# Two transformer blocks on one core: block 2's products at 512 columns, full-row scores, one root at the entry, the selector's units last, and norm 2 in pairs

## The chip, the cores and the metric

The kernel runs on one core of one Trainium2 chip. The metric is device microseconds of one execution of the whole program. The kernel before took 2176.15, 2176.34 and 2179.45 us in three runs; the median is 2176.34 us.

## The reference

Everything is fp32; there are 256 tokens of width 2048. Block 1 is one layer: eight stick-breaking heads (sb), eight sparse heads (dsa) whose keys a small indexer selects, and a gated FFN with a causal convolution of width 3 and inner width 5504. Block 2 is two layers, each with three kinds of attention on one normalized input: six "fox" heads (a forget gate), six "mla" heads (low-rank, with a 64-wide rope part that all heads share) and four "diff" heads (two 64-wide maps each, subtracted); each output is gated, and one product leads back to width 2048. Cut to the lines that the change touches:

```python
h = rmsnorm(x, norm1_g[l]) * (1.0 + sc1) + sh1
rel = jax.nn.relu(jnp.einsum('bqhd,bkd->bqhk', q_idx[:, start:end], k_idx[:, :L]))   # 16 indexer heads of 64
_, sel = lax.top_k(score, topk)
x = x + g1 * (merged @ w_out[l])
h2 = rmsnorm(x, norm2_g[l]) * (1.0 + sc2) + sh2
x = x + g2 * conv_ffn(h2, w_up[l], conv_w[l], conv_b[l], w_down[l])
# block 2, mla: 128 + 64 rows per score
s = (jnp.einsum('bqhd,bkhd->bhqk', q_nope[:, q0:q1], k_nope[:, :q1])
     + jnp.einsum('bqhr,bkr->bhqk', q_rope[:, q0:q1], k_rope[:, :q1]))
# block 2, diff: two maps of 64 rows
s1 = jnp.einsum('bqhd,bkhd->bhqk', q1[:, q0:q1_], k1[:, :q1_]).astype(jnp.float32) * scale + bias
s2 = jnp.einsum('bqhd,bkhd->bhqk', q2[:, q0:q1_], k2[:, :q1_]).astype(jnp.float32) * scale + bias
```

## The kernel before

Weights come from HBM in steps of 512 KB (128 rows by 1024 columns). For accuracy each is split on the chip into a high and a low part: ACT copies the high part (`wh`, L1731), DVE subtracts for the low part (`wl`, L1740). Activations have such pairs too (`a0h`, `a0l` and so on). A product of a 128x128 weight block with 256 tokens is three matmuls of 256 columns: wh with the high part, wh with the low part, wl with the high part (`mm_feature`, L516; `mm_token`, L537, for values with tokens in the rows). I call these three, for one block of 128 rows (k) and one of 128 columns (m), a pair. In the FFN `mm_halves` makes a pair of one matmul of 512 columns (wh with high and low side by side, L527) and one of 256 (L528). A unit is 256 output columns with all 16 row blocks, so 32 pairs in four steps; it fills one of two PSUM banks named `mm`, which ACT or DVE empties one step later.

Stages by time in the profiled execution: input product of block 1 20 to 365 us, output product 368 to 479, norm 2 479 to 489, FFN 489 to 1219, block 2's layer 0 1219 to about 1690, layer 1 to 2158, and the final norm.

Attention is side work: generators on three lanes (PSUM tiles `l0a`, `l0b`, `l1a` ...), each of which issues one part of its work between two steps of the products. An engine runs its instructions in the order written, so a matmul of a side job that waits holds up the products behind it. `IN_PASSES` sets in which order the units of block 1's input product are finished: the indexer's (0 to 5), the dsa queries (5 to 10), the sb heads.

Places that the change touches: `scores` (L786) issues a head's score products, for 128 tokens against 128 keys and for 128 against 256; mla adds a second pair for the 64 rows of `krd` and `qr`. `indexer` L744 does 64-row products, two tiles side by side. `h2_tiles` (L1098 to L1100) makes the input of the FFN from `xa`, which ACT scales at L1076. `first_rs` runs at block 2's entry: two sums of squares (L606, L607) and two chained inverse roots, since block 1's final norm and block 2's first norm follow on each other. `fm_evac` (L1372, L1374) empties a unit's bank in one DVE operation of 512 columns.

## Time and profile before

| | |
|---|---|
| median of three runs | 2176.34 us |
| the profiled execution: time, span | 2171.6 us, 2169.8 us |
| TensorE (PE) busy | 2118.1 us (98%) |
| VectorE (DVE) busy | 1514.3 us (70%) |
| ScalarE (ACT) busy | 1138.9 us (52%) |
| GpSimd (POOL) busy | 91.0 us (4%) |
| HBM | 211 GB/s over the span |

Busy time of matmuls overlaps from one to the next, so the pace is read from the distance of two starts, not from the length of one. A row of the timeline gives start, length, engine, line, operation, tiles and shape; consecutive alike instructions share a row, and a bracket at its end tells how long the engine had been idle before it and on whose work it waited.

### The profile page before, as it was taken

The page shows a single profiled execution, that of the slowest core. Times are in us where ns is not written, and L with a number is a line of the kernel's source. Part 1 is how long each engine was busy: PE and PEld are TensorE (multiplying, and loading weights), DVE is VectorE, ACT ScalarE, POOL GpSimd, SP SyncE. Part 2 cuts the span into 40 slices and gives each one's busy share as a digit, 9 for nine tenths or more (in the row PEclk, how much of TensorE's full clock was granted, in tenths as well). Part 3 has the DMA queues.
Part 4 walks back from the last instruction along what each step waited for, and adds up shares of the span by engine and source line. Part 5 has one row for each costly group of instructions (what it writes and reads, how often), then busy time and mean ns, then how long its engine had stood idle before and what let it go on. Part 6 is the DMA issues. An engine that isn't in the chain of part 4 may idle for free.

```text
span 2169.8 us, 39066 instructions
## 1 busy us (share of the span) xinstructions
PE 2118.1 (98%) x15435; PEld 1958.2 (90%) x15435; DVE 1514.3 (70%) x2495; ACT 1138.9 (52%) x1810; POOL 91.0 (4%) x87
## 2 busy tenths in 40 slices
PE   8999899999999999999999999999999999999997
PEld 6898789988888888888888899998999999998997
DVE  8596858989988678877778855476555545675654
ACT  5876446444565455535555535464544444554543
POOL 0000000011200000000001200000001100000000
PEclk9999999999999999999999999999999999999999
DMA  9999687777855777776655555544455655544552
GB/s 344 357 358 359 222 305 255 249 260 282 273 193 185 227 225 234 231 244 224 199 175 184 166 186 169 174 135 152 147 179 157 200 184 159 161 131 146 178 182 98
DMA packets 131821, 460.48 MB, mean 212 GB/s; under 512 B 15655, under 2 KB 17591, under 8 KB 131637
## 3 DMA queue, kind: packets, MB, share of 16 engines
q1 hardware_dynamic: 128736, 453.27, 62.8%
q0 software_dynamic: 2176, 4.30, 0.8%
q8 instruction: 121, 1.98, 0.4%
q14 instruction: 64, 0.52, 0.1%
q10 hardware_dynamic: 724, 0.41, 0.1%
HBM read 455.80 MB, written 2.90 MB: 211 GB/s over the span
## 4 chain that ended last, share of the span: by engine, by line
PE 50%; DVE 2%; issue 1%; ACT 0%; DMA 0%; POOL 0%; DVEq 0%; ACTq 0%; POOLq 0%
PE mm L516 32%; PE mm L537 6%; PE mm L527 3%; PE l1b L527 2%; PE l1a L527 2%; PE mm L528 1%; PE l1a L528 1%; PE l1b L528 1%; DVE wl L1740 1%; PE l0a L786 1%; PE l2a L786 1%; PE l1a L786 1%; DMA t<-t5d 0%; DVE XT L1675 0%; ACT l_t L778 0%
## 5 line engine op out<-in xcount | busy, mean ns | idle before, releaser
L1740 DVE TENSOR_TENSOR wl<-raw,wh 128x1024 fp32r<-128x1024 f32 (+4 forms) x697 | 830.7, 1198 | 443.6 <-PE mm L516 216.3
L1731 ACT ACTIVATE wh<-raw 128x1024 fp32r<-128x1024 f32 (+4 forms) x697 | 705.3, 1017 | 624.9 <-PE mm L516 276.2
L456 DVE CUSTOM_DVE_ANT_0 ada<-ada,CROW 128x1024 f32<-128x1024 f32 x128 | 156.1, 1227 | 3.8 <-DMA ada<-in_weights_dram 3.6
L516 PE MATMUL mm<-mix,wh 128*128 128x256 f32 x512 | 93.6, 285 | 0.3 <-DVE wo L1063 0.3
L516 PEld LDWEIGHTS mm<-mix,wh 128*128 128x128 f32 x512 | 79.8, 192 | 0.5 <-issue 0.4
L516 PE MATMUL mm<-mix,wl 128*128 128x256 f32 x256 | 72.6, 284 | 1.2 <-DVE wl L1740 1.2
L778 ACT ACTIVATE l_t<-l_t,l_mx 128x128 f32<-128x128 f32 x96 | 43.0, 448 | 51.0 <-DVE l_mx L776 51.0
L516 PE MATMUL mm<-a6h,wh 128*128 128x256 f32 (+2 forms) x242 | 52.2, 297 | 0.0
L516 PE MATMUL mm<-a4h,wh 128*128 128x256 f32 (+2 forms) x242 | 50.4, 299 | 1.3 <-ACT mm L985 1.1
L1050 POOL COPY sqacc<-sq 128x512 f32<-128x512 f32 x4 | 4.0, 990 | 1111.1 <-ACT sq L1045 1111.1
L516 PEld LDWEIGHTS mm<-mix,wl 128*128 128x128 f32 x256 | 49.0, 192 | 1.6 <-DVE wl L1740 1.6
L1052 POOL TENSOR_TENSOR sqacc<-sqacc,sq 128x512 f32<-128x512 f32 x25 | 40.4, 1617 | 203.8 <-ACT sq L1045 203.8
L516 PE MATMUL mm<-a7l,wh 128*128 128x256 f32 (+2 forms) x242 | 48.7, 283 | 0.0
L516 PE MATMUL mm<-a7h,wh 128*128 128x256 f32 (+2 forms) x242 | 48.7, 283 | 0.0
L516 PE MATMUL mm<-a6l,wh 128*128 128x256 f32 (+2 forms) x242 | 48.7, 283 | 0.0
L516 PE MATMUL mm<-a5l,wh 128*128 128x256 f32 (+2 forms) x242 | 47.1, 284 | 0.5 <-ACT a5l L646 0.4
L516 PE MATMUL mm<-a5h,wh 128*128 128x256 f32 (+2 forms) x242 | 47.1, 285 | 0.0
L516 PE MATMUL mm<-a4l,wh 128*128 128x256 f32 (+2 forms) x242 | 47.0, 285 | 0.0
L516 PEld LDWEIGHTS mm<-a4h,wh 128*128 128x128 f32 (+2 forms) x242 | 37.9, 189 | 4.3 <-ACT mm L985 1.9
L1162 ACT ACTIVATE fy<-fu,PC 128x256 f32<-128x256 f32 x60 | 32.8, 594 | 15.1 <-DVE fu L1138 15.1
L516 PEld LDWEIGHTS mm<-a6h,wh 128*128 128x128 f32 (+2 forms) x242 | 37.7, 190 | 3.2 <-issue 1.6
L516 PEld LDWEIGHTS mm<-a5l,wh 128*128 128x128 f32 (+2 forms) x242 | 37.9, 192 | 1.0 <-ACT a5l L646 0.6
(1512 smaller groups left out, 6751.8 us busy)
## 6 DMA issues: line engine op xcount, KB each, us to landing
raw<-in_weights_dram SPq DMA_DIRECT2D x638, 512.0 KB, 4.0
ada<-in_weights_dram SPq DMA_DIRECT2D x192, 512.0 KB, 5.2
raw<-in_weights_dram SPq DMA_DIRECT2D x30, 256.0 KB, 2.6
raw<-in_weights_dram SPq DMA_DIRECT2D x8, 384.0 KB, 3.1
XT<-in_x_dram SPq DMA_DIRECT2D x4, 512.0 KB, 6.1
out_dram<-XT SPq DMA_DIRECT2D x8, 256.0 KB, 2.4
l_t<-nd POOLq DMA_DIRECT2D x12, 128.0 KB, 4.9
raw<-in_weights_dram SPq DMA_DIRECT2D x8, 140.0 KB, 2.1
```

The lines of the kernel that those rows point to most:

```text
L456: DVE.tensor_tensor_reduce(raw, raw, CROW[:, 1024 * g : 1024 * (g + 1)], 1.0, 0.0, ALU.mult, ALU.add, SUMS[:, h, j, g : g + 1])
L516: PE.matmul(o, a[:, j, wsl], b, start=first and j == 0 and m == 0 and x == 0, stop=last and j == len(ks) - 1 and x == 2, skip_group_check= ...
L527: PE.matmul(ps[0][m], wh[:, j, msl], act.both(ks[j]), start=first and j == 0, stop=False, skip_group_check=True)
L528: PE.matmul(ps[0][m][:, 1, :], wl[:, j, msl], act.H(ks[j]), start=False, stop=end, skip_group_check=True)
L537: PE.matmul(ps[0][:, tt, :n], a[:, tsl], b[:, j, :n], start=first and j == 0 and tt == 0 and x == 0, stop=last and j == len(ks) - 1 and x ...
L778: ACT.activation(Pt[:, a:b], Pt[:, a:b], AF.Exp, bias=mx[:, qt : qt + 1], scale=-1.0, accum_out=sm[:, qt : qt + 1])
L786: PE.matmul(z[:, a:b], q[:, qt * P : (qt + 1) * P], k[:, : b - a], start=x == 0, stop=x == len(pairs) - 1)
L1050: nc.gpsimd.tensor_copy(acc, sq)
L1052: nc.gpsimd.tensor_tensor(acc, acc, sq, ALU.add)
L1162: ACT.activation(y[:, m], ps[:, m, :], AF.Identity, bias=col("conv_b", c), scale=col("conv_w2", c))
L1731: ACT.activation(h, a, AF.Copy)
L1740: DVE.tensor_tensor(l, a, h.bitcast(F32), ALU.subtract)
```

## The change

- Block 2's products of the queries, keys, low-rank parts, gates and outputs (all units of feature form but the small one and `aq0`: 20 a layer, and 8 of `wo`) become `half_unit`: first all 16 row blocks of columns 0 to 127, then those of 128 to 255. Each pair is one matmul of 512 and one of 256 columns, and each half has a bank of its own, which `half_evac` empties in three operations of 256 columns.
- Scores in 128 rows: for mla and diff ACT copies the query with one half of its rows multiplied by zero, and the key stays whole; the indexer's key is stored twice with zeros in the other half. In block 1 the two products of value tile 0 become one.
- `first_rs` takes one root for the product of both norms, and spawns two steps later.
- The units of the selector are finished last in block 1's input product; the dsa heads wait for them.
- Norm 2: `xa` is scaled by POOL instead of ACT; `h2_tiles` goes by pairs, on DVE alone, in place.

```diff
--- before.py
+++ after.py
-             (0, 5, 8, 12, "put"), (17, 22, 4, 8, "put"), (5, 10, 8, 12, "put"), (0, 5, 12, 16, "put"), (5, 10, 12, 16, "put"), (10, 17, 8, 16, "put"), (17, 22, 8, 16, "put"))
+             (0, 5, 8, 12, "put"), (17, 22, 4, 8, "put"), (5, 10, 8, 12, "put"), (5, 10, 12, 16, "put"), (0, 5, 12, 16, "put"), (10, 17, 8, 16, "put"), (17, 22, 8, 16, "put"))
...
-H2_TILES = (0, 4, 5, 8)
+H2_TILES = (0, 4, 6, 8)
...
+    HALVES = [kcol[:, 4 + j : 5 + j] for j in range(2)]
...
+    def mm_half(ps, act, ks, first, last):
+        def go(wh, wl):
+            h, l = (w.rearrange("p k n -> p (k n)").rearrange("p (k n) -> p k n", n=P) for w in (wh, wl))
+            for j, k in enumerate(ks):
+                PE.matmul(ps[0], h[:, j, :], act.both(k), start=first and j == 0, stop=False, skip_group_check=True)
+                PE.matmul(ps[0][:, 1, :], l[:, j, :], act.H(k), start=False, stop=last and j == len(ks) - 1, skip_group_check=True)
+        return go
+    def half_unit(loads, ks, act, evac, pre=None):
+        for m in range(2):
+            ps = [None]
+            at = [(max(o, m * P), o, w, name, row, c) for o, w, name, row, c in loads if o < (m + 1) * P and o + w > m * P]
+            for i in range(0, len(ks), 8):
+                pk = ks[i : i + 8]
+                first, last = i == 0, i + 8 >= len(ks)
+                core = mm_half(ps, act, pk, first, last)
+                def mm(wh, wl, ps=ps, first=first, core=core):
+                    if first:
+                        ps[0] = pp.tile([P, 2, T], F32, tag="mm", bufs=2, name="mm")
+                    core(wh, wl)
+                parts = [(len(pk), P, [(a - m * P, min(o + w, (m + 1) * P) - a, name, row + pk[0] * P, c + a - o) for a, o, w, name, row, c in at])]
+                steps.append(Step(parts, mm, (lambda ps=ps, m=m: evac(ps[0], m)) if last else None, pre if m == 0 and i == 0 else None))
...
+        for j in range(2):
+            DVE.memset(kix[rows[1 - j], j, :], 0.0)
...
-                    po = 64 * j
-                    PE.matmul(ps[j][:, m, :n], S[f"qix{g}"][po : po + 64, m, tsl], kix[po : po + 64, :n], start=True, stop=True)
+                    PE.matmul(ps[j][:, m, :n], S[f"qix{g}"][:, m, tsl], kix[:, j, :n], start=True, stop=True)
...
-        PE.matmul(o[:, 0:P], v(0), PT[:, 0, :], start=True, stop=True)
-        PE.matmul(o[:, P:T], v(0), PT[:, 1, :], start=True, stop=False)
-        PE.matmul(o[:, P:T], v(1), PT[:, 2, :], start=False, stop=True)
+        PE.matmul(o, v(0), PT[:, 0:2, :].rearrange("p a b -> p (a b)"), start=True, stop=False, skip_group_check=True)
+        PE.matmul(o[:, P:T], v(1), PT[:, 2, :], start=False, stop=True, skip_group_check=True)
...
+            side.spawn("dsa", lambda L, h=h: dsa_head(L, h), after=("rds", "qix", "idx"))
...
-                        ACT.activation(G["xa"][k // 2][:, k % 2], XT[:, k, :], AF.Copy, scale=a2[:, k : k + 1])
+                        nc.gpsimd.tensor_scalar(G["xa"][k // 2][:, k % 2], XT[:, k, :], a2[:, k : k + 1], None, op0=ALU.mult)
...
-        for k in range(lo, hi):
-            t = ring("ht", (P, T))
-            (nc.gpsimd if k % 2 else DVE).tensor_tensor(t, G["xa"][k // 2][:, k % 2], G["RS2"], ALU.mult)
-            ACT.activation(H2.H(k), t, AF.Identity, bias=mod(3, k))
-            DVE.scalar_tensor_tensor(H2.L(k), t, mod(3, k), H2.H(k).bitcast(F32), op0=ALU.add, op1=ALU.subtract)
+        for k0 in range(lo, hi, 2):
+            xa, rs = G["xa"][k0 // 2], G["RS2"]
+            if k0 == 0:
+                for j in range(2):
+                    DVE.tensor_tensor(xa[:, j], xa[:, j], rs, ALU.mult)
+                    ACT.activation(H2.H(j), xa[:, j], AF.Identity, bias=mod(3, j))
+            else:
+                DVE.tensor_tensor(xa, xa, b2(rs), ALU.mult)
+                for j in range(2):
+                    ACT.activation(H2.H(k0 + j), xa[:, j], AF.Identity, bias=mod(3, k0 + j))
+            for j in range(2):
+                DVE.scalar_tensor_tensor(H2.L(k0 + j), xa[:, j], mod(3, k0 + j), H2.H(k0 + j).bitcast(F32), op0=ALU.add, op1=ALU.subtract)
...
+        RSX = G["rsx"] = cp.tile([P, T], F32, tag="RSa", name="RSX")
+        m1, m2 = L.sb("t2", [P, T]), L.sb("t3", [P, T])
+        ACT.copy(m1, ps)
+        DVE.scalar_tensor_tensor(m2, m1, EPS, ps2, op0=ALU.mult, op1=ALU.add)
+        rsqrt(L, RSX, m2, D, squared=True)
         r1 = cp.tile([P, T], F32, tag="RSb", name="r1")
-        rsqrt(L, r1, ps, D)
-        q = L.sb("t2", [P, T])
-        DVE.tensor_tensor(q, r1, r1, ALU.mult)
-        yield
-        r2 = cp.tile([P, T], F32, tag="RSc", name="r2")
-        RSX = G["rsx"] = cp.tile([P, T], F32, tag="RSa", name="RSX")
-        rsqrt(L, r2, ps2, D, pre=q)
-        DVE.tensor_tensor(RSX, r1, r2, ALU.mult)
         side.spawn("rsc", lambda L: rs_cols(L, RSX, rsx, 3), after=("rsx",))
-        side.spawn("x2", lambda L: second_x(L, r1))
+        side.spawn("x2", lambda L: second_x(L, r1), after=("rsx",))
+        yield
+        rsqrt(L, r1, m1, D)
...
+        def half_evac(name, i, RS, scale=None, then=None):
+            def ev(ps, m):
+                if m == 0:
+                    S2[name] = i() if callable(i) else slot(i, name)
+                s = S2[name]
+                t = ring("half", (P, T))
+                ACT.activation(t, ps[:, 0, :], AF.Copy, scale=1.0 if scale is None else scale)
+                if scale is None:
+                    DVE.tensor_tensor(t, ps[:, 1, :], t, ALU.add)
+                else:
+                    DVE.scalar_tensor_tensor(t, ps[:, 1, :], scale, t, op0=ALU.mult, op1=ALU.add)
+                DVE.tensor_tensor(s[:, m], t, RS(), ALU.mult)
+                if then and m == 1:
+                    then(s)
+            return ev
...
-            po = slice(64 * (h % 2), 64 * (h % 2) + 64)
-            qr = S2[f"qr{h // 4}"][po, (h // 2) % 2, :]
+            qr = L.sb("t1", [P, T])
+            ACT.activation(qr, S2[f"qr{h // 4}"][:, (h // 2) % 2, :], AF.Copy, scale=HALVES[h % 2])
+            yield
             z = L.ps("a", [P, 384])
-            scores(z, [(qn[:, h % 2, :], kn), (qr, S2["krd"][po])])
+            scores(z, [(qn[:, h % 2, :], kn), (qr, S2["krd"])])
...
+            qz = L.sb("t1", [P, 2, T])
+            for j in range(2):
+                ACT.activation(qz[:, j], q[:, h % 2, :], AF.Copy, scale=HALVES[j])
+            yield
             for j in range(2):
                 z = L.ps("ab"[j], [P, 384])
-                po = slice(64 * j, 64 * j + 64)
-                scores(z, [(q[po, h % 2, :], k[po, h % 2, :])])
+                scores(z, [(qz[:, j], k[:, h % 2, :])])
...
-             pre=lambda: (opened(), side.spawn("rsx", first_rs if l == 0 else layer_rs)), pre_at=3, delay=3)
+             pre=opened, pre_at=3, delay=3)
         for j in range(3):
-            unit(mat(W, O_AQ + 256 * j, 256), 256, kd, H, fm_evac(f"aq{j}", j, RSX, scale=P**-0.5))
+            if j == 0:
+                unit(mat(W, O_AQ, 256), 256, kd, H, fm_evac("aq0", 0, RSX, scale=P**-0.5),
+                     pre=lambda: side.spawn("rsx", first_rs if l == 0 else layer_rs), pre_at=1)
+                continue
+            half_unit(mat(W, O_AQ + 256 * j, 256), kd, H, half_evac(f"aq{j}", j, RSX, scale=P**-0.5))
...
-            unit(mat(W, off + 256 * j, 256), 256, kd, H, fm_evac(f"g{i}", WHERE[i], RSX, then=then), pre=pre)
+            half_unit(mat(W, off + 256 * j, 256), kd, H, half_evac(f"g{i}", WHERE[i], RSX, then=then), pre=pre)
...
+                def ev(ps, j):
+                    m = 2 * u + j
+                    for h in range(2):
+                        DVE.tensor_tensor(XT[:, m, :], XT[:, m, :], ps[:, h, :], ALU.add)
+                    split((XA[1].H(m), XA[1].L(m)), XT[:, m, :], scale=col("norm_g_2", 16 + m))
+                    if j:
+                        add_sq(sq1, XT[:, 2 * u : 2 * u + 2, :], u)
                 return ev
...
-                unit(mat(WO, 256 * u_, 256), 256, kd, M, wo_evac(u_), pre=wait_gates if u_ == 0 else None)
+                half_unit(mat(WO, 256 * u_, 256), kd, M, wo_evac(u_), pre=wait_gates if u_ == 0 else None)
```

On PE at block 2's entry, before: `sqacc`, `sq` are the sums of squares that POOL folds, `a0h` to `a7l` the input tiles, and the 70-column unit is the small one.

```order
L516 MATMUL mm<-a5h,wl 70x256
L516 MATMUL mm<-a5l,wh 70x256 x2
L516 MATMUL mm<-a5l,wl 70x256
L606 MATMUL l0b<-sqacc,ones 128x256
L607 MATMUL l0b<-sqacc,ones 128x256
L606 MATMUL l0a<-sq_122,ones 128x256
L607 MATMUL l0a<-sq_122,ones 128x256
L516 MATMUL mm<-a6h,wh 70x256 x2
L516 MATMUL mm<-a6h,wl 70x256
```

After, the small unit's end runs straight into `aq0`:

```order
L520 MATMUL mm<-a7h,wl 70x256
L520 MATMUL mm<-a7l,wh 70x256 x2
L520 MATMUL mm<-a7l,wl 70x256
L520 MATMUL mm<-a0h,wh 128x256 x2
L520 MATMUL mm<-a0h,wl 128x256
```

And, still after, the end of the first step of `aq0` with the products of `first_rs`:

```order
L520 MATMUL mm<-a1l,wh 128x256 x2
L520 MATMUL mm<-a1l,wl 128x256
L637 MATMUL l0b<-sqacc,ones 128x256
L638 MATMUL l0b<-sqacc,ones 128x256
L637 MATMUL l0a<-sq_127,ones 128x256
L638 MATMUL l0a<-sq_127,ones 128x256
L520 MATMUL mm<-a2h,wh 128x256 x2
L520 MATMUL mm<-a2h,wl 128x256
```

The four products with `ones` stood ahead of the last two of the small unit's eight pairs of tiles in its last step, and now stand behind the first step of `aq0`.

On PE around the first mla score of a layer, before (`kn`, `qn` are the key and query of 128 rows, `krd`, `qr` the rope parts in 64):

```order
L537 MATMUL mm<-wh,m5l 128x256 x2
L537 MATMUL mm<-wl,m5l 128x256
L786 MATMUL l1a<-kn_15972,qn_15822 128x128
L786 MATMUL l1a<-krd,qr_15921 128x128
L786 MATMUL l1a<-kn_15972,qn_15822 128x256
L786 MATMUL l1a<-krd,qr_15921 128x256
L516 MATMUL mm<-a0h,wh 128x256 x2
L516 MATMUL mm<-a0h,wl 128x256
```

After, where `l_t` is ACT's copy of the query with half its rows zero:

```order
L568 MATMUL mm<-wh,m5l 128x256 x2
L568 MATMUL mm<-wl,m5l 128x256
L820 MATMUL l0a<-kn_15649,qn_15499 128x128
L820 MATMUL l0a<-krd,l_t_15731 128x128
L820 MATMUL l0a<-kn_15649,qn_15499 128x256
L820 MATMUL l0a<-krd,l_t_15731 128x256
L540 MATMUL mm<-a0h,wh 128x512
L541 MATMUL mm<-a0h,wl 128x256
```

The number of score products is the same; the rope's are 128 rows deep, and the unit behind them is in pairs of 512 and 256 columns.

On PE at the end of block 1's input product, before (`qsb`, `ksb` belong to an sb head, `vds` is the dsa heads' value, and `mix` is the input of the output product):

```order
L537 MATMUL mm<-wh,a7l 128x256 x2
L537 MATMUL mm<-wl,a7l 128x256
L867 MATMUL l0a<-l_t_4233,sbk 128x256
L868 MATMUL l0a<-l_t_4233,sbk 128x128
L869 MATMUL l0a<-l_t_4233,sbk 128x128
L854 MATMUL l1a<-qsb_603,ksb_558 128x256
L855 MATMUL l1a<-qsb_603,ksb_558 128x128
L857 MATMUL l1a<-sbk,c_ident 128x128 x2
L875 MATMUL l0b<-l_t_4333,vsb_556 128x256
L876 MATMUL l0b<-l_t_4333,vsb_556 128x128
L854 MATMUL l2a<-qsb_603,ksb_558 128x256
```

After, from the last step of the input product to the last dsa head:

```order
L568 MATMUL mm<-wh,a7l 128x256 x2
L568 MATMUL mm<-wl,a7l 128x256
L887 MATMUL l0a<-qsb_511,ksb_509 128x256
L888 MATMUL l0a<-qsb_511,ksb_509 128x128
L890 MATMUL l0a<-sbk,c_ident 128x128 x2
L826 MATMUL l1a<-c_ident,l_t_4178 128x128 x3
L832 MATMUL l1b<-l_t_4291,vds 128x256
L833 MATMUL l1b<-l_t_4291,vds 128x128
```

The dsa heads' last transposes (L826) and value product (L832, L833) now stand behind the input product, directly one after the other. On ACT stands there, in the changed kernel (`l_t` from `l0a` to the third row is the sb head's):

```order
L894 ACTIVATE l_t_4285<-l0a 128x384
L895 ACTIVATE l_t_4285<-l_t_4285 128x384
L896 ACTIVATE l_t_4285<-l_t_4285,kcol 128x384
L829 COPY l_t_4291<-l1a 128x384
L839 ACTIVATE mix_4236<-l1b,PC 128x256
```

The copy (L829) that lies between the transposes and the value product has three operations of the sb head ahead of it.

## Rows read from the trace of the kernel before

**Rows 1.** The page: busy time, share of the span, instructions of each engine.

```profile
PE 2118.1 (98%) x15435; PEld 1958.2 (90%) x15435; DVE 1514.3 (70%) x2495; ACT 1138.9 (52%) x1810; POOL 91.0 (4%) x87
```

**Rows 2.** Waits of PE in block 2: total us, times, longest us.

```profile
PE mm L516 <- DVE wl L1740: 1.9, 1, 1.9
...
PE l0b L606 <- POOL sqacc L1052: 1.3, 1, 1.3
```

**Rows 3.** Waits of PE in the indexer's stretch, 222 to 285 us.

```profile
PE l0b L744 <- ACT l_t L748: 2.0, 1, 2.0
PE l2b L744 <- ACT l_t L748: 1.9, 2, 1.4
PE l2a L744 <- ACT l_t L748: 1.9, 1, 1.9
PE mm L537 <- DVE wl L1740: 1.2, 1, 1.2
```

**Rows 4.** Timeline of PE in block 2's layer 0: start us, length us.

```profile
1301.75 0.40 PE L537 MATMUL mm<-wh,a0h 128*128 128x256 f32 x2
...
1305.71 0.40 PE L537 MATMUL mm<-wh,a2l 128*128 128x256 f32 x2
```

**Rows 5.** Timeline of PE in the FFN, 900 to 906 us.

```profile
901.08 0.39 PE L527 MATMUL mm<-m0h,wh 128*128 128x512 f32 x1
...
905.24 0.39 PE L527 MATMUL mm<-m3h,wh 128*128 128x512 f32 x1
```

**Rows 6.** Timeline of PE in the FFN, 1060 to 1066 us.

```profile
1060.72 0.40 PE L527 MATMUL l1a<-a0h,wh 128*128 128x512 f32 x1
...
1064.96 0.40 PE L527 MATMUL l1a<-a3h,wh 128*128 128x512 f32 x1
```

**Rows 7.** Timeline of PE around an mla head's scores.

```profile
1500.63 0.28 PE L537 MATMUL mm<-wl,m5l 128*128 128x256 f32 x1
...
1503.08 0.28 PE L516 MATMUL mm<-a0h,wl 128*128 128x256 f32 x1
```

**Rows 8.** Timeline of PE around a fox head's scores.

```profile
1322.43 0.28 PE L537 MATMUL mm<-wl,a5l 128*128 128x256 f32 x1
...
1323.45 0.28 PE L537 MATMUL mm<-wl,a6h 128*128 128x256 f32 x1
```

**Rows 9.** Timeline of PE around a diff head's scores.

```profile
1406.49 0.28 PE L537 MATMUL mm<-wl,a1l 128*128 128x256 f32 x1
1406.70 0.37 PE L786 MATMUL l0a<-dk,dq 64*128 64x128 f32 x1
1406.71 0.37 PE L786 MATMUL l0b<-dk,dq 64*128 64x128 f32 x1
...
1407.90 0.28 PE L537 MATMUL mm<-wl,a2h 128*128 128x256 f32 x1
```

**Rows 10.** Groups on ACT, 226 to 368 us: count, busy us, mean ns, idle before.

```profile
L862 ACT ACTIVATE l_t<-l_t 128x384 f32<-128x384 f32 x3 | 1.6, 525 | 0.1
```

**Rows 11.** Timeline of ACT, DVE and POOL around norm 2.

```profile
473.63 3.30 ACT L1076 ACTIVATE xa<-XT,a 128x256 f32<-128x256 f32 x8
477.91 1.23 DVE L1740 TENSOR_TENSOR wl<-raw,wh 128x1024 fp32r<-128x1024 f32 x1 [3.69 <-ACT wh L1731]
481.90 0.48 DVE L1063 SCALAR_TENSOR_TENSOR wo<-mm,MOD,RSs 128x256 f32<-128x256 f32 x1
487.93 0.43 DVE L1098 TENSOR_TENSOR ht<-xa,RS 128x256 f32<-128x256 f32 x1
489.92 0.96 DVE L1098 TENSOR_TENSOR ht<-xa,RS 128x256 f32<-128x256 f32 x1
546.01 1.89 POOL L642 TENSOR_SCALAR ht<-ht,a 128x256 f32<-128x256 f32 x1
```

**Rows 12.** Busy us of PE, PEld, DVE, ACT, POOL; clock; DMA share; GB/s, in block 2.

```profile
1430.00:1455.00 25.00, 24.15 (x198) 23.68 (x198) 20.79 (x46) 15.64 (x34) 0.00 (x0) 1.00 0.45 144
```

**Rows 13.** Groups on DVE in layer 0: the emptying of a gate's unit.

```profile
L1372 DVE TENSOR_TENSOR g<-mm,RSX 128x512 f32<-128x512 f32 x6 | 4.1, 687 | 3.4 <-PE mm L516 3.4
```

More of the change, by code (lines that the diff above doesn't have):

```diff
@@ L242, in views @@
         at, k0, out = 0, 0, []
+        if len(self.parts) == 1 and self.parts[0][1] == P and self.parts[0][0] == 8:
+            return [(raw, split.rearrange("p k n -> p (k n)"))]
         whole = all(n == T for _, n, _ in self.parts)
@@ L718, in small1 @@
         s = S["small"]
-        yield from rope_dup(L, kix, s[:, 0, :], DUPI, DUPX, COSI, SINI)
+        rows = (slice(0, 64), slice(64, P))
+        for j in range(2):
+            DVE.memset(kix[rows[1 - j], j, :], 0.0)
+        yield from rope_dup(L, [(rows[j], kix[:, j, :]) for j in range(2)], s[:, 0, :], DUPI, DUPX, COSI, SINI)
         ps = L.ps("b", [P, 2, 16])
```

69 lines of the change are left out of this document (34 added, 35 removed).

## The prediction

> **What bounds the kernel now.** I read the page's busy times first: PE is busy for 2118.1 us, 98% of the span [rows 1], so a change pays only where it takes time out of PE's own stream or out of one of its few waits. Then I read PE's waits by stretch. In block 2, the only stretch in which products change, the waits that I count on are one of 1.9 us for DVE's weight split and one of 1.3 us for POOL's sums of squares, both at the entry [rows 2]; around the indexer they are 5.8 us for ACT's relu and 1.2 us for a weight split [rows 3]. Last I read the pace of the products from the timeline. DVE and ACT matter where they come near to full: DVE is busy for 20.79 of 25 us in the fullest stretch of block 2, ACT for 15.64 [rows 12].
>
> **The pairs of block 2.** A pair of three 256-column products takes (1305.71 - 1301.75)/11 = 0.360 us [rows 4]. The FFN shows the new form at two paces: (905.24 - 901.08)/12 = 0.3467 us [rows 5] and (1064.96 - 1060.72)/12 = 0.3533 us [rows 6]. So a pair saves 13.3 or 6.7 ns. The change converts 28 units of 32 pairs in each of two layers, 1792 pairs, which is 23.8 or 12.0 us. No row tells which of the two block 2 will get. Its stream is broken by a side job every few steps, and a broken stream is not likely to keep the better pace, so I lean to the slow one, three eighths of the way to the fast: -12.0 - 0.375 x 11.8 = -16.4 us. Both ends stay in the range.
>
> **Scores in 128 rows.** From the third product's start before a job to that behind it I take off the three products of 0.120 us between. An mla head then costs 1503.08 - 1500.63 - 0.36 = 2.09 us [rows 7], a fox head, with one full-depth product per block of scores instead of two, 1323.45 - 1322.43 - 0.36 = 0.66 [rows 8]. If an mla head of full depth throughout costs two fox heads, 1.32, each of 12 heads saves 0.77: -9.2 us. The fox row is the nearest there is; the bounds are nothing and this. A diff head now runs its two 64-row maps side by side (l0a and l0b start 10 ns apart) and costs 1407.90 - 1406.49 - 0.36 = 1.05 us [rows 9]. Two full-depth maps one behind the other are two fox heads, 1.32: +0.27 for 8 heads, +2.2. The indexer's eight rounds hold as many score columns as eight diff heads (four products a round, of 256 columns in four rounds and of 128 in the other four: 6144, against 2 x 384 in a diff head), so +2.2 there too. The masks are ACT copies one step ahead (0.41 us for 256 columns by 3.30/8 [rows 11]), 28 in all, beside products that last over 2 us a step; I count them in the waits below. The value products keep their columns: 0.
>
> The Trainium skill (TensorEngine Tiling (Array Packing), Key Properties) says that a change of tiling mode drains TensorE; the mla row, where full and half depth alternate, agrees with 2.09 against 1.32. The same page (Theoretical Speedup) gives tiles of 64 rows up to twice the speed, which speaks against the change for diff and indexer: by it the maps side by side would have taken 0.66, and the loss would be 8 x 0.66 = 5.3 us each instead of 2.2. The row with 1.05 decides.
>
> **The entry.** The four ones-products and the chain of roots behind them move past `aq0`'s first step, and one root replaces two in sequence. POOL has its sums ready by then, and DVE splits weights before it does roots: both waits go, -3.2 us. What is late next is the emptying of the small unit, which needs RSX: it has the two further steps, over 5 us, and I count nothing.
>
> **The selector.** With its units last, the indexer no longer meets the queries' ropes on DVE, which were ahead of its own operations there. All waits of its stretch would go: -5.8 and -1.2. The dsa heads come later for it, and the last one is left over behind the input product: its transposes are directly followed by its value product, with an ACT copy between that has three operations of the sb head ahead of it. Four such operations at about 0.525 us [rows 10] are 2.1 us in which PE has nothing else in its queue: +2 (0 to 4, if the lot repeats once).
>
> **Norm 2.** DVE waits 3.69 us for the weights' high part, because ACT does eight scalings for 3.30 us first [rows 11]. On POOL they no longer stand there, so the last units of the output product, and with them the sums of squares and the root, come up to 3.3 us earlier. The cost is beside it: POOL takes 1.89 us for one such scaling, 15.1 us for eight, and next to POOL the same DVE product takes 0.96 instead of 0.43 us [rows 11]. I take -2.5 (-4 with the pairs, +1 if DVE's stretching eats it).
>
> The Trainium skill (SBUF — State Buffer, Who interferes with whom) says that a DVE instruction with two inputs in SBUF and a GpSimd instruction that reads SBUF exclude each other for the whole of one. The 0.96 against 0.43 agrees. It is rival C.
>
> **New waits in block 2.** A half's bank must be empty before the next but one half starts: 16 pairs, 5.6 us, where a unit of 32 pairs left 11.5. Behind a half's end lie one ACT copy (0.41), a DVE operation from PSUM (0.48) and one from SBUF (0.43) [rows 11], 1.3 us, with a weight split of 1.23 on DVE and one on ACT possibly ahead: about 3.7 of 5.6 us. DVE does 1.8 us per unit where it did 0.687 [rows 13], 1.1 us more in 11 us: 20.79 becomes some 23 of 25 in the fullest stretch, and there it may run late. At the end of each layer the first half of `wo` reaches the last gate's rows after 14 pairs, 4.9 us, where both halves' pairs stood ahead of them before, some 10. I take +3 (0 to 8).
>
> **Sum.** -16.4 - 9.2 + 2.2 - 3.2 - 7.0 + 2.2 + 2 - 2.5 + 3 = -28.9 us. The profiled execution took 2171.6 us (its span is 2169.8), so 2142.7; the median of the runs is 4.7 us above it, so 2147.4: about 2147.
>
> **Rivals.**
>
> A, the pace does not change: in block 2 the 512-column pairs settle at 0.360 us. For it: the slow FFN pace is only 6.7 ns better [rows 6], and block 2's stream is broken more often. Against: both stretches of the FFN are below 0.360 [rows 5, 6]. Time: 2147 + 16.4 = 2164. Chance 7%.
>
> B, full depth is not what mla lacked: the cost of 2.09 is that of a second operand pair, not of the half depth. For it: no row shows two full-depth pairs in one head. Against: a second set of the same columns should cost what the first did. Time: 2147 + 9.2 = 2157. Chance 6%.
>
> C, POOL and DVE exclude each other in norm 2: before norm 2's root DVE does some seven operations with two SBUF inputs (three splits, four additions), each of which would wait for up to one POOL operation of 1.89 us [rows 11]; half of that on average is +6.6, and the -2.5 is gone. Time: 2147 + 9.1 = 2156. Chance 6%. Against: POOL's operations would fall partly in DVE's idle 3.69 us.
>
> D, the other side: the halves' emptying. Each of the 112 halves is emptied by three operations on two engines, in the order in which they stand behind weight splits and softmax work. If PE waited for a bank 0.26 us on average, the whole gain of 28.9 would be gone; at 0.5 us the time is 2147 + 56 = 2203. For it: a unit's 11.5 us are halved, and DVE nears full [rows 12]. Against: 3.7 of 5.6 us, and the row is the fullest, not the usual one. Chance 5%.
>
> **How the numbers follow.** My forecast has 76%, A 7%, B 6%, C 6%, D 5%. The forecast's own ends: the fast pace (-7.4), no new waits (-3), no wait behind the input product (-2) and norm 2 at its best (-1.5) lead to 2133; new waits of 8 (+5), 4 us behind the input product (+2) and norm 2 at +1 (+3.5) to 2158. Since these do not come together, 2131 to 2161 holds it with most of B and C and leaves out A's upper part and D. A measurement here can tell about 0.2%, 4.4 us, from no change: below 2172 is faster. The forecast and A to C all lie there; of D and of mishaps of several kinds together I put 4% within the bound and 5% above it, which leaves 91% for faster.
>
> **What would show it.** In the changed kernel's timeline, twelve 512-and-256 pairs in block 2 take 4.16 or 4.24 us; 4.32 is A. An mla head costs about 1.3 us between products; 2.1 is B. A diff head costs 1.3. The waits list of block 2 lacks POOL's sums and the 1.9 us at the entry, and has few entries where a product into `mm` waits for `half_evac`'s DVE operations; over a hundred are D. Around the indexer no waits for its relu remain, and one or two of about 2 us stand between input and output product. In norm 2 DVE's idle 3.69 us is gone and the FFN starts earlier; DVE additions of 1 us and more there are C. The forecast is wrong if the sum of new waits exceeds 20 us, or if a pair's pace stays at 0.360.

## The result and the profile after

The changed kernel took 2150.57 us (median of four runs, 2148.54 to 2152.52), the kernel before 2176.65 in its four; the ratio is 0.988 with a 95% interval of 0.9864 to 0.9896. The forecast was 2147, the range 2131 to 2161. The profiled execution of the changed kernel has a span of 2150.7 us, 19.1 less than before; the medians differ by 26.1, because the profile of before was one of its quickest executions and that of the changed kernel the slowest of its four. The two paces of the FFN, below, are a likely reason; the executions without a profile can't show it.

Read from the first and last products of each stage in the timelines:

| stage | before, us | after, us | difference |
|---|---|---|---|
| up to the first product | 20.95 | 21.46 | +0.5 |
| input product with the heads, to the output product | 347.61 | 348.52 | +0.9 |
| output product | 110.50 | 110.25 | -0.3 |
| norm 2, to the first FFN product | 10.41 | 8.05 | -2.4 |
| FFN | 729.70 | 733.49 | +3.8 |
| block 2 | 938.87 | 917.12 | -21.8 |
| tail | 11.71 | 11.78 | +0.1 |

One profile of a kernel is not exact to the tenth. Ten of the profiles taken have the changed kernel's code up to the output product (the changed kernel, experiments 1, 2, 4 to 7 and 9 to 11), and there the heads' stretch took 346.2 to 349.5 us, 347.7 in the mean. Six have its block 2 (the changed kernel, experiments 3, 6, 7, 9 and 11): 914.0 to 917.1 us. So a difference of 1 us in either row tells nothing.

The page after, busy time by engine (answers to [rows 1]):

```profile
PE 2101.3 (98%) x13563; PEld 1868.6 (87%) x13563; DVE 1564.3 (73%) x2669; ACT 1169.6 (54%) x1911; POOL 102.7 (5%) x91
```

PE lost 16.8 us of work and is as full as before. DVE has 50 us more, nearly all for the halves' emptying (experiment 1, without halves, has 1517.5 us).

Block 2's pairs, timeline of PE, two stretches of twelve pairs each (answer to [rows 4]):

```profile
1270.02 0.40 PE L540 MATMUL mm<-a4h,wh 128*128 128x512 f32 x1
...
1274.26 0.40 PE L540 MATMUL mm<-a2h,wh 128*128 128x512 f32 x1
...
1600.34 0.39 PE L540 MATMUL mm<-m4h,wh 128*128 128x512 f32 x1
...
1604.50 0.39 PE L540 MATMUL mm<-m2h,wh 128*128 128x512 f32 x1
```

4.24 and 4.16 us: both paces of the FFN stand in block 2, 353.3 and 346.7 ns a pair. Over its 1647 undisturbed pairs the mean is 348.75, so 1792 pairs save 1792 x 11.25 ns = 20.2 us.

An mla head and a diff head, timeline of PE (answer to [rows 7, 9]):

```profile
1406.99 0.28 PE L568 MATMUL mm<-wl,a3l 128*128 128x256 f32 x1
1407.12 0.82 PE L820 MATMUL l0a<-dk,l_t 128*128 128x128 f32 x4
...
1408.66 0.29 PE L568 MATMUL mm<-wl,a4h 128*128 128x256 f32 x1
...
1504.35 0.28 PE L541 MATMUL mm<-a3l,wl 128*128 128x256 f32 x1
...
1504.69 0.39 PE L820 MATMUL l1a<-krd,l_t 128*128 128x128 f32 x2
...
1506.01 0.28 PE L541 MATMUL mm<-a4h,wl 128*128 128x256 f32 x1
```

The diff head costs 1408.66 - 1406.99 - 0.36 = 1.31 us, the mla head 1506.01 - 1504.35 less a pair of 0.353 = 1.31. Both were forecast as 1.32.

Waits of PE in block 2 (total us, times, longest us; answer to [rows 2]):

```profile
PE l2a L1560 <- ACT l_t L1557: 4.4, 2, 2.2
PE mm L520 <- DVE wl L1810: 1.6, 1, 1.6
PE mm L568 <- DVE kn L1415: 1.3, 2, 0.7
PE mm L568 <- ACT bv L1443: 0.6, 2, 0.3
PE l0b L1348 <- DVE RSK L344: 0.6, 2, 0.3
```

The wait for POOL's sums is gone, that for the split at the entry only shrank from 1.9 to 1.6. No product waits for a bank of the halves. But the sum over a diff head's squares, which waited 0.9 us in each layer, waits 2.2. Before, its row read:

```profile
PE l2a L1497 <- ACT l_t L1494: 1.7, 2, 0.9
```

And it costs more than the wait. First the window of PE behind the first of these waits in the changed kernel, then that behind the same wait (2.21 us) in experiment 6, whose code in block 2 is the same (the columns are us, then busy us of PE, PEld, DVE, ACT, POOL, granted clock, DMA share, GB/s):

```profile
1444.00:1447.40 3.40, 3.39 (x10) 2.82 (x11) 3.33 (x5) 1.79 (x3) 0.00 (x0) 0.52 0.34 108
```

```profile
1442.85:1446.25 3.40, 3.40 (x19) 2.97 (x20) 3.34 (x5) 1.68 (x3) 0.00 (x0) 1.00 0.33 87
```

For 3.4 us the granted clock is 0.52, so PE runs at the lower of its levels, 1.2 GHz, after it stood still for 2.2 us: it issues 10 products where experiment 6 issues 19. The loss can be measured. Six profiles have this code, so twelve such waits. Behind five the clock fell, and the next 500 products took 81.3 to 81.5 us; behind seven it stayed at 1.00, and they took 79.8 to 80.0. A fall costs 1.5 us here, and whether it comes is not set by the length of the wait, which was 2.16 to 2.22 us in all twelve. In the changed kernel's profile the clock fell behind both, at 1444 and at 1900. That accounts for block 2's spread: 914.0 us in the profile with no such stretch, 915.4 to 915.6 in those with one, 917.0 and 917.1 in those with two (one of these may stand behind the wait at the entry).

Between input and output product stand such waits too. First the waits of PE there (200 to 372 us, answer to [rows 3]), in the changed kernel and two rows of before, then the timeline, then windows: behind the first stop, and before, in and behind the second:

```profile
PE l1b L832 <- ACT l_t L829: 4.3, 2, 2.2
PE mm L520 <- ACT mm L1021: 2.5, 2, 1.4
```

```profile
PE mm L516 <- ACT mm L985: 1.1, 1, 1.1
PE l1b L798 <- ACT l_t L795: 0.7, 1, 0.7
```

```profile
343.68 0.70 PE L832 MATMUL l1b<-l_t,vds 128*128 128x256 f32 x2 [2.19 <-ACT l_t L829]
...
361.93 1.06 PE L832 MATMUL l1b<-l_t,vds 128*128 128x256 f32 x2 [2.08 <-ACT l_t L829]
...
366.55 0.59 PE L908 MATMUL l2b<-l_t,vsb 128*128 128x256 f32 x2
```

```profile
345.05:348.45 3.40, 3.40 (x18) 3.40 (x18) 2.95 (x6) 1.75 (x5) 0.00 (x0) 0.50 0.96 280
...
357.00:359.85 2.85, 2.85 (x23) 2.56 (x22) 1.25 (x3) 2.77 (x6) 0.00 (x0) 1.00 0.94 266
359.85:361.90 2.05, 0.00 (x0) 0.00 (x0) 1.21 (x2) 1.97 (x5) 0.00 (x0) 1.00 0.34 106
361.95:365.60 3.65, 3.65 (x12) 3.20 (x13) 1.06 (x3) 1.29 (x3) 0.00 (x0) 0.53 0.34 130
366.20:369.00 2.80, 2.80 (x20) 2.60 (x19) 1.57 (x4) 1.69 (x4) 0.00 (x0) 1.00 0.00 0
```

The indexer's waits for its relu are gone, all of them. In their place the dsa value product waits twice for its copy on ACT, 2.19 us at 343.68 and 2.08 us at 361.93, and behind each the clock falls: behind the first 1.4 us later, at 345.07, behind the second at once, so that the value product takes 1.06 us where an sb head's of the same shape takes 0.59 at 366.55.

What these two falls cost can be read from the ten profiles with this code. Behind the first wait the clock fell in six and stayed at 1.00 in four. The second wait was 2.0 to 2.1 us in the six and 3.6 in the four, and its end stood 18.24 to 18.26 us behind the end of the first in all ten. So this fall cost nothing: the end of the second wait isn't set by PE's pace, and what PE loses at half clock it waits less. From the second wait's end to the output product it was 8.03 or 8.04 us in the seven profiles in which the clock fell there, and 6.91 in the other three: this fall cost 1.1 us.

Norm 2, timelines of POOL and DVE (answer to [rows 11]):

```profile
476.53 9.27 POOL L1112 TENSOR_SCALAR xa<-XT,a 128x256 f32<-128x256 f32 x8
```

```profile
475.88 1.76 DVE L1810 TENSOR_TENSOR wl<-raw,wh 128x1024 fp32r<-128x1024 f32 x1 [0.50 <-ACT wh L1801]
...
486.19 1.32 DVE L1136 TENSOR_TENSOR xa<-xa,RS 128x256 f32<-128x256 f32 x2
```

DVE's idle 3.69 us became 0.50. POOL needs 9.27 us for the eight, 1.16 each and not 1.89. Beside it a split takes 1.76 instead of 1.23 us, but most DVE operations there are as long as ever.

The FFN, which the change touches only at its start, twelve pairs (answer to [rows 5]):

```profile
900.86 0.40 PE L531 MATMUL l1b<-a5l,wh 128*128 128x512 f32 x1
...
905.10 0.40 PE L531 MATMUL mm<-m0l,wh 128*128 128x512 f32 x1
```

4.24 us where it was 4.16 at the same place. The mean of the undisturbed pairs of the FFN is 352.7 ns after and 349.4 before; over 2064 pairs that is 6.8 us, of which fewer and shorter stops give 3.0 back. The code is the same but for its start: what differs is how much of it ran at which of the two paces.

### The profile page after: what moved, and what is told of

The parts are those of the page before. It is cut to its first block, busy times and chain, and to the rows that moved or that the text cites. A ratio compares the mean times of both kernels' runs of the same rounds, so it can differ in the third digit from the quotient of the medians.

```text
span 2150.7 us, 35556 instructions
## 1 busy us (share of the span) xinstructions
PE 2101.3 (98%) x13563; PEld 1868.6 (87%) x13563; DVE 1564.3 (73%) x2669; ACT 1169.6 (54%) x1911; POOL 102.7 (5%) x91
## 4 chain that ended last, share of the span: by engine, by line
PE 82%; DVE 11%; ACT 3%; DMA 3%; issue 2%; DVEq 0%; SPq 0%; ACTq 0%
PE mm L540 19%; PE mm L531 11%; PE mm L520 9%; PE mm L541 9%; PE mm L568 6%; PE mm L532 5%; PE l1a L531 5%; PE l1b L531 5%; DVE wl L1810 3%; DVE ada L460 3%; PE l1a L532 3%; PE l1b L532 3%; DMA ada<-in_weights_dram 2%; PE l0a L415 1%; ACT wh L1801 1%
## 5 line engine op out<-in xcount | busy, mean ns | idle before, releaser
L1810 DVE TENSOR_TENSOR wl<-raw,wh 128x1024 fp32r<-128x1024 f32 (+5 forms) x697 | 824.3, 1188 | 372.1 <-PE mm L541 128.2
L1801 ACT ACTIVATE wh<-raw 128x1024 fp32r<-128x1024 f32 (+5 forms) x697 | 705.6, 1017 | 578.0 <-PE mm L540 160.4
L540 PE MATMUL mm<-a0h,wh 128*128 128x512 f32 x80 | 36.3, 454 | 0.0
L1208 DVE SCALAR_TENSOR_TENSOR fy<-fu,PC,fy 128x255 f32<-128x255 f32 x60 | 28.9, 481 | 10.2 <-ACT fy L1205 10.2
L540 PE MATMUL mm<-a4h,wh 128*128 128x512 f32 x80 | 35.4, 443 | 0.0
L1428 ACT ACTIVATE half<-mm 128x256 f32<-128x256 f32 x80 | 29.3, 366 | 8.8 <-PE mm L541 8.8
L540 PE MATMUL mm<-a5l,wh 128*128 128x512 f32 x80 | 32.2, 402 | 0.0
L540 PE MATMUL mm<-a6l,wh 128*128 128x512 f32 x80 | 32.0, 400 | 0.0
L540 PE MATMUL mm<-a4l,wh 128*128 128x512 f32 x80 | 31.9, 399 | 0.0
L540 PE MATMUL mm<-a7l,wh 128*128 128x512 f32 x80 | 31.9, 399 | 0.0
```

What stands on the lines that cost most here:

```text
L540: PE.matmul(ps[0], h[:, j, :], act.both(k), start=first and j == 0, stop=False, skip_group_check=True)
L1801: ACT.activation(h, a, AF.Copy)
L1810: DVE.tensor_tensor(l, a, h.bitcast(F32), ALU.subtract)
```

## The experiments

Theory: the gain is the pairs (20 us), mla's depth (9 us) and norm 2 (2.4 us); what was lost went to four waits of about 2 us, each with half clock behind it, and the selector's move is worth nothing for that reason. (That every fall of the clock costs time is what the ten profiles above speak against.) Rivals stand with each experiment. All edits are to the changed kernel; stage times are read as in the table above.

**1. Whole units again in block 2.**

```diff
-            half_unit(mat(W, O_AQ + 256 * j, 256), kd, H, half_evac(f"aq{j}", j, RSX, scale=P**-0.5))
+            unit(mat(W, O_AQ + 256 * j, 256), 256, kd, H, fm_evac(f"aq{j}", j, RSX, scale=P**-0.5))
...
```

> The changed kernel with block 2's half units back as whole units of 256-column products and one evacuation each (outputs included); all else as changed. Theory: the pairs give 20 us (11 ns for each of 1792, a mix of both paces), and the added emptying costs some 5 us of waits and slow clock at the diff heads, so this takes 2150.6 + 13 to 20 = 2164 to 2171, and block 2 shows 1.0 us or less per diff wait. Rival (the halves' emptying eats the gain): 2151 or less.

2164.45 us (2160.95 to 2166.54), ratio to before 0.9939 [0.992, 0.9957]. Block 2 takes 931.46 us, 14.3 more; the wait at the diff sums falls from 4.4 to 1.9 us in all, and block 2 has no stretch at half clock behind them. Against the 914.0 to 917.1 us of the unchanged block it is 14.3 to 17.4 more. So the pairs, 20 us by their own starts, are worth 14 to 17 net, and 3 to 6 go back, part of it to the longer diff waits and the half clock; that the emptying alone takes it was not separated. The rival falls.

**2. The mla rope in 64 rows.**

```diff
-            qr = L.sb("t1", [P, T])
-            ACT.activation(qr, S2[f"qr{h // 4}"][:, (h // 2) % 2, :], AF.Copy, scale=HALVES[h % 2])
-            yield
+            po = slice(64 * (h % 2), 64 * (h % 2) + 64)
+            qr = S2[f"qr{h // 4}"][po, (h // 2) % 2, :]
```

> The changed kernel with the mla rope scores back in 64 rows, without the mask and its extra step. Theory: each of 12 heads costs 2.09 us again instead of 1.31, so +9 us: 2160. Rival (a second operand pair is what costs, not its depth): 2151, and a head still costs 1.3 to 2.1 in both forms alike.

2158.65 us (2156.48 to 2159.95), ratio 0.9918 [0.9898, 0.9938]. Block 2 takes 926.36 us, +9.2. That this agrees with the forecast to a tenth is luck. The profile has one half-clock stretch more than the changed kernel's, at the entry; without its 1.5 us the difference would be some 7.8. The edit also takes out the mask and its step. The rival (rival B of the prediction) falls: it is the depth.

**3. The selector's units in the old place.**

```diff
-             (0, 5, 8, 12, "put"), (17, 22, 4, 8, "put"), (5, 10, 8, 12, "put"), (5, 10, 12, 16, "put"), (0, 5, 12, 16, "put"), (10, 17, 8, 16, "put"), (17, 22, 8, 16, "put"))
+             (0, 5, 8, 12, "put"), (17, 22, 4, 8, "put"), (5, 10, 8, 12, "put"), (0, 5, 12, 16, "put"), (5, 10, 12, 16, "put"), (10, 17, 8, 16, "put"), (17, 22, 8, 16, "put"))
...
-            side.spawn("dsa", lambda L, h=h: dsa_head(L, h), after=("rds", "qix", "idx"))
+            side.spawn("dsa", lambda L, h=h: dsa_head(L, h), after=("rds", "idx"))
```

> The changed kernel with the selector's units finished in the old place; its products stay in 128 rows. Theory: the indexer's three waits for its relu (5.9 us) come back, and the two waits of 2.1 to 2.2 us for the copy ahead of the dsa value product go, each with about 2 us of half clock behind it; the two nearly cancel: 2148 to 2152, and from the first product to the output product about 347 to 350 us as against 348.5. Rival (finishing the selector last gains its 7 us, and the loss is elsewhere): 2157.

2147.78 us (2145.93 to 2151.39), ratio 0.9871 [0.985, 0.9892]: not told apart from the changed kernel by the whole time. The stretch takes 347.63 us, 0.9 less than the changed kernel's profile and inside the spread of its code. Its waits (222 to 372 us):

```profile
PE l2b L778 <- ACT l_t L782: 1.4, 1, 1.4
PE l2a L778 <- ACT l_t L782: 1.3, 1, 1.3
...
PE l0b L778 <- ACT l_t L782: 1.0, 1, 1.0
PE l1b L832 <- ACT l_t L829: 0.7, 1, 0.7
```

The indexer's waits return smaller, 3.7 us and not 5.8, and the long ones of the dsa value product go. The move gained nothing that these profiles can tell; theory holds, but for the half clock in it.

**4. One more step ahead of the diff heads' sum.**

```diff
             ACT.activation(sq, o, AF.Square)
             yield
+            yield
             ps = L.ps("a", [P, T])
```

> The changed kernel with one more step between a diff head's square and its sum over rows on TensorE. Theory: the two waits of 2.2 us at 1444 and 1900 go, and with them the half clock that follows each for 2 to 3 us (some 1.5 us each): 2143 to 2146. Rival (the half clock comes from something else): the waits go but the clock rows of 0.57 and 0.69 stay, 2146 to 2147.

2150.32 us (2146.96 to 2152.07), ratio 0.9879 [0.9858, 0.9899]. The waits named are gone, and block 2 takes 916.38, 0.7 less than in the changed kernel's profile and inside the spread of its code, since others came, as the waits of block 2 show:

```profile
PE l0b L832 <- ACT l_t L829: 2.9, 2, 1.5
PE l0b L1348 <- DVE RSK L344: 1.7, 2, 0.8
```

Neither forecast held: the head's tail is one step later, a diff value product now waits 1.5 us for its copy in each layer, and the low-rank part behind it 0.8. Behind the second of these value products, at 1907 us, the clock fell once more. The step only moved the waiting; that ACT and DVE are full there fits with this, but wasn't tested by itself.

**5. The diff maps in 64 rows.**

```diff
-            qz = L.sb("t1", [P, 2, T])
-            for j in range(2):
-                ACT.activation(qz[:, j], q[:, h % 2, :], AF.Copy, scale=HALVES[j])
-            yield
             for j in range(2):
                 z = L.ps("ab"[j], [P, 384])
-                scores(z, [(qz[:, j], k[:, h % 2, :])])
+                po = slice(64 * j, 64 * j + 64)
+                scores(z, [(q[po, h % 2, :], k[po, h % 2, :])])
```

> The changed kernel with the diff heads' maps back in 64 rows side by side, without masks and without their extra step. Theory: each of eight heads costs 1.05 us again instead of 1.31, -2.1 us, and ACT and DVE lose 16 copies and a shift of phase at the gates, so the two waits of 2.2 us at the diff sums shrink to about 1 us and their half clock goes: block 2 takes 917.1 - 2 to 7 us, the whole 2144 to 2149. Rival (full depth is as good there): block 2 at 917, the whole 2150 to 2152.

2145.99 us (2145.58 to 2146.55), ratio 0.9857 [0.9839, 0.9874]. Block 2 takes 912.36, 4.8 less. By the rows 2.1 of it is the scores; the rest is at the sums, whose waits and clock read:

```profile
PE l2a L1557 <- ACT l_t L1554: 2.3, 2, 1.2
```

```profile
1436.00:1446.00 10.00, 8.83 (x52) 7.59 (x51) 8.96 (x17) 6.11 (x12) 0.00 (x0) 1.00 0.46 152
```

The wait is 1.2 us at most and the clock stays at 1.00. The changed kernel's profile had two falls of 1.5 us here, which make up the rest; against experiment 9, whose block 2 is the changed kernel's without a fall (914.0), this edit gains 1.7 us. So for diff the change lost by its products, which stand one behind the other and had run side by side, and by a diff wait of 2.2 us, behind which the clock fell in half of the cases. How much of that wait is the masks on ACT and how much the extra step, one edit can't tell; experiment 1 shortens it too, to 1.0 us, with both kept.

**6. Norm 2's scalings on ACT.**

```diff
-                        nc.gpsimd.tensor_scalar(G["xa"][k // 2][:, k % 2], XT[:, k, :], a2[:, k : k + 1], None, op0=ALU.mult)
+                        ACT.activation(G["xa"][k // 2][:, k % 2], XT[:, k, :], AF.Copy, scale=a2[:, k : k + 1])
```

> The changed kernel with norm 2's eight scalings on ACT again, the tiles still in pairs. Theory: the gain of norm 2 (10.4 us before, 8.05 after, from the output product's end to the first FFN product) was the free ACT: DVE's wait of 3.7 us for the weights' high part returns, and the stretch takes 10 us or more, the whole 2152 to 2153. Rival (the pairs gave it): the stretch stays near 8 us, the whole 2150.

2149.94 us (2146.89 to 2154.84), ratio 0.9877 [0.9857, 0.9898], too wide to tell. The stretch from the output product's end to the first FFN product takes 10.54 us (10.41 before, 8.05 in the change): the gain is the free ACT, the pairs give nothing there. DVE's idle time ahead of the split is back:

```profile
477.06 1.23 DVE L1810 TENSOR_TENSOR wl<-raw,wh 128x1024 fp32r<-128x1024 f32 x1 [3.70 <-ACT wh L1801]
```

**7. Small jobs inside the FFN.** For the two paces, 346.7 and 353.3 ns.

```diff
+        if n_wout + 30 <= i < n_ffn and (i - n_wout) % 8 == 0:
+            kind = "ABCD"[(i - n_wout) // 8 % 4]
+            if kind in "AD":
+                po = side.lanes[2].ps("a", [P, T])
+                PE.matmul(po, ones, G["RS2"], start=True, stop=False, skip_group_check=True)
+                PE.matmul(po[:, P:T], ones, ones, start=False, stop=True, skip_group_check=True)
+            if kind in "AB":
+                pt = side.lanes[2].ps("b", [P, 3, P])
+                for j in range(3):
+                    PE.transpose(pt[:, j, :], ones, ident)
+            if kind == "C":
+                PE.matmul(side.lanes[2].ps("a", [P, T])[:, :P], ones, ones, start=True, stop=True)
         st.mm(*bufs.pop(i))
```

> The changed kernel with a small extra job on TensorE ahead of every eighth step of the FFN, four kinds in turn, whose results nothing reads: A an fp32 product of 256 and one of 128 columns and three transposes, B three transposes, C one fp32 product of 128 columns, D A without transposes. Theory: the two paces of a pair (346.7 and 353.3 ns) are set anew at each interruption, by its kind; in block 2 the pace was the fast one after every one of 20 places with A's sequence. So after A all stretches are at 346.7, after B, C and D either. Rival (the pace is drawn at random or drifts with time): A's stretches are slow as often as others. The extra work is about 29 jobs of 0.3 to 1 us, 15 to 20 us in all.

2162.86 us (one run). A stretch behind each job, timeline of PE: job A and twelve pairs, then job B and twelve pairs:

```profile
673.37 0.59 PE L1875 MATMUL l2a<-RS,ones 128*128 128x256 f32 x2
...
674.02 0.49 PE L1880 MATMUL l2b<-c_ident,ones 128*128 128x128 f32 x3
...
675.05 0.39 PE L531 MATMUL l1a<-a0l,wh 128*128 128x512 f32 x1
...
679.21 0.39 PE L531 MATMUL l1a<-a3l,wh 128*128 128x512 f32 x1
```

```profile
695.85 0.49 PE L1880 MATMUL l2b<-c_ident,ones 128*128 128x128 f32 x3
...
696.88 0.40 PE L531 MATMUL l1a<-m0l,wh 128*128 128x512 f32 x1
...
701.12 0.40 PE L531 MATMUL l1a<-m3l,wh 128*128 128x512 f32 x1
```

4.16 us behind A, 4.24 behind B. Behind A the pace was the fast one 8 times of 8, behind B and D the slow one 15 of 15, behind C fast in 2 of 7. So the pace is not drawn at random; behind A it is the fast one each time, in experiments 9 and 10 below behind a fast stretch too. B always came behind a fast stretch and D mostly behind a slow one, so of these two it isn't shown that they set it by themselves. Theory holds as far as A.

**8. Edits 3 and 5 together.**

```diff
-             (0, 5, 8, 12, "put"), (17, 22, 4, 8, "put"), (5, 10, 8, 12, "put"), (5, 10, 12, 16, "put"), (0, 5, 12, 16, "put"), (10, 17, 8, 16, "put"), (17, 22, 8, 16, "put"))
+             (0, 5, 8, 12, "put"), (17, 22, 4, 8, "put"), (5, 10, 8, 12, "put"), (0, 5, 12, 16, "put"), (5, 10, 12, 16, "put"), (10, 17, 8, 16, "put"), (17, 22, 8, 16, "put"))
...
-                scores(z, [(qz[:, j], k[:, h % 2, :])])
+                scores(z, [(q[po, h % 2, :], k[po, h % 2, :])])
```

> The changed kernel with the selector's units in the old place and the diff maps in 64 rows. Theory: the two edits stand in different stretches and add up: -1 to -3 and -2 to -7 us, 2141 to 2147. Rival (their gains are in the spread of the pace of the FFN): 2148 to 2151.

2149.28 us (2146.05 to 2149.74), ratio 0.9873 [0.9855, 0.9891], above edit 5 alone and in the rival's range. In its profile block 2 takes 912.36 as in 5, and the stretch of the heads 348.25. The edits don't add up: 3 has no gain of its own beyond the spread.

**9, 10. Job A at four places; the same with edit 5.**

```diff
+        if i - n_wout in (3, 27, 176, 190):
+            cols, turns = [((256, 128), 3)][0]
...
         st.mm(*bufs.pop(i))
```

> The changed kernel with the extra job A (fp32 products of 256 and 128 columns and three transposes, results unread) ahead of FFN steps 3, 27, 176 and 190, that is behind each place where the FFN's stream is interrupted anyway. Theory (A sets the fast pace): all 2064 pairs but some 15 at 346.7 ns, the FFN takes 733.5 - 12.5 + 4 = 725 us in every run, the whole about 2142, with less spread. Rival (the pace is drawn anew for other reasons): FFN 733 to 738, the whole 2150 to 2154.

> The changed kernel with the diff maps in 64 rows and the four jobs A in the FFN. Theory: both gains add, 2146.0 - 8 = 2138. Rival (diff's gain was the pace of the FFN in its runs): 2142 as with the jobs alone.

2146.58 us (2145.92 to 2149.39), ratio 0.9867 [0.9849, 0.9886], and 2144.42 us (2143.2 to 2145.12), ratio 0.9853 [0.9838, 0.9867]. The last has the lowest time of all versions, but its interval overlaps that of experiment 5. Both FFNs take 732.0 us, not 725, which lies within the 729.8 to 734.6 of the profiles without jobs: behind each job the pace is fast, but after the second it turns slow again at about 606 us, without a stop, in both, and stays so until the third job. Neither theory's sizes hold, and a turn without a stop is not covered by it; its cause stays open.

**11. Four other jobs.**

```diff
+            cols, turns = [((256,), 3), ((128,), 3), ((256, 128), 1), ((), 1)][(i - n_wout) // 8 % 4]
...
```

> The changed kernel with four other extra jobs in turn ahead of every eighth step of the FFN: an fp32 product of 256 columns and three transposes; one of 128 and three transposes; A with one transpose; one transpose alone. Theory (transposes behind an fp32 product set the pace): the first three are always followed by 346.7 ns, the fourth not always. Rival (the length of the job decides, modulo some period): each kind maps pace to pace in its own way, and one or more of the first three are followed by 353.3. About 29 jobs of 0.4 to 0.9 us, 2155 to 2170.

2163.33 us (one run). The first three kinds were followed by the fast pace 2 of 8, 5 of 8 and 2 of 7 times, the fourth 4 of 7. The theory falls; none of these sets the pace as A does. Nor does each kind map pace to pace, as the rival had it: behind a slow stretch the first kind was followed by either. What in A sets it stays open.

**12. Edit 5, A at 3, 45 and 184, and a later dsa value product.**

```diff
         ACT.copy(PT, pt)
         yield
+        if late:
+            yield
         o = L.ps("b", [P, T])
```

> The changed kernel with the diff maps in 64 rows, one more step between a dsa head's transposes and its value product, and job A ahead of FFN steps 3, 45 and 184 (45 instead of 27 and 176: with A at 27 the pace turned slow at step 41 without a stop). Theory: the two waits of 2 us and more for the copy ahead of the dsa value product and their half clock go (from the first product to the output product 343 to 346 us instead of 347.2), and the FFN is fast from step 45 on (726 to 729 us instead of 732); the whole 2137 to 2142. Rival (a wait only moves, and the pace turns slow again by itself): 2143 to 2147, with waits of the same sum elsewhere in the stretch and the FFN at 732.

2148.63 us (2148.03 to 2150.26), ratio 0.9869 [0.9852, 0.9885]. Above both forecasts. The stretch of the heads takes 351.5 us, and its waits read (200 to 380 us):

```profile
PE l1b L858 <- DVE sqo L848: 4.3, 1, 4.3
PE l1a L826 <- DVE l_t L872: 2.3, 1, 2.3
PE mm L568 <- ACT mm L1023: 2.2, 1, 2.2
```

The waits for the copy went, as the theory had it, but others came for them, as the rival had it, and their sum grew from 7.1 to 10.4 us. The heads end a step later, so that their sum of squares stands behind the input product with nothing beside it. The FFN (731.3 us) turned slow at 686 us, behind a hesitation of 0.3 us.

## Why the prediction was right, point by point

- **The pairs**: forecast -16.4, measured -20.2 by the starts (experiment 1: 14 to 17 of it net). The mechanism was right; the share of the fast pace was seven tenths ((353.3 - 348.75)/6.6) and not three eighths. That a stream often broken keeps the slow pace was a guess without a row, and it is wrong: A's sequence, a value product and transposes, is just what the heads put there.
- **mla** -9.2: right in mechanism, shown by its rows and by experiment 2; the size is 8 to 9. **Diff** +2.2: the scores cost that (1.31 against 1.05). Experiment 5's other 2.7 us are, within the noise, the two falls of the clock behind the diff sums, counted below; the prediction priced no wait beyond its length.
- **The entry** -3.2: measured -1.6. POOL's wait went; the split is still late, and why was not tried. In four of the profiles (experiments 1, 2, 6 and 11) the clock fell behind this wait of 1.6 us as well.
- **The selector and what is left over behind it**: forecast -7.0 + 2.2 + 2 = -2.8, measured +0.9 in the profile. With the old order the stretch took 347.6 us before, 347.6 in experiment 3 and 348.3 in 8, with the new one 347.7 in the mean of ten: nothing is gained. This is the step that failed, at its +2 for what is left over. The indexer's waits for its relu went as forecast, and the 2.2 for its deeper products fits (experiment 3, in the old order, has 1.8 us less of waits than before and is as long). The wait behind the input product came by the mechanism forecast, the copy on ACT behind an sb head's operations. That it was 2.08 for 2.1 us is luck, since it is 3.6 in four profiles of the same code. But a second such wait came at 343.68, where the copy stands on ACT behind another head's softmax and that waits for DVE's other work, and ACT's copies into `mm` are waited for 1.4 us longer: of the 7.0 us of waits only 2.3 were gained (9.4 in all before, 7.1 after). The fall of the clock behind the input product added 1.1, that behind the wait at 343.68 nothing. (Before had one such stretch too, behind the indexer's last waits.)

  The selector's units aren't last of all, as the text ahead of the prediction has it: they are finished behind the dsa queries and ahead of the sb heads. The indexer's products ran from 226 to 258 us before and from 248 to 273 in the changed kernel; the dsa heads, which wait for them, start at 298 instead of 289 us, and their last value product stands at 363 instead of 357.

- **Norm 2** -2.5: measured -2.4, by the mechanism named (experiment 6). Rival C did not come: POOL was through in 9.3 us.
- **New waits in block 2** +3: measured 2.7 at the diff sums, 3.0 by half clock behind them, 1.2 others: 6.9 in this profile, and 3.9 where the clock stays. The diff sums stood in the list of before with 1.7 us; the prediction didn't name them, and looked for late DVE work at the banks. No half waited for a bank; rival D fell at its first condition.
- The errors cancelled in part: -3.8 in the pairs against +3.7 in the selector, +3.9 in the waits and +1.6 at the entry, 5.4 us left over. The FFN's +3.8 in the profile isn't the change's. That the median came within 4 us of the forecast is luck to that extent: the stages of the profiles say 19.1 us gained, the medians 26.1, and the forecast was 28.9.

## What to carry to other kernels

Price a wait of TensorE by its length and by what follows it: behind the diff sums a wait of 2.2 us was followed by a fall of the clock in half of the cases, worth 1.5 us. But ask what PE waits for next: behind the wait at 343.68 the same fall cost nothing, since the next wait ended when it did anyway. Fill TensorE's rows where a product of half depth stands alone between full ones, as in mla, and not where two of half depth run side by side, as in diff. Move work to the engine that is idle in that stretch, not on average, as in norm 2. When a full engine's wait is moved by a step, look for it at the next place before counting it as gained. And take the spread of a stage from profiles in which its code is the same before reading a microsecond from one of them.
